# Two groups of TensorE transposes as pairs of half transposes in a hybrid SSD and attention layer

## The chip, the cores and the metric

The kernel runs on one core of a Trainium2 chip. The metric is device time in microseconds (us), the median of several executions; less is better. PE is TensorE's matmul side and PEld its loading of weights, DVE is VectorE, ACT is ScalarE, POOL is GpSimd, SP is the engine that issues the transfers here.

## The reference

One post-norm layer over 512 tokens of width 1024, in float32. Cut to what matters for the change:

```python
u = h @ w_in                        # z | x,B,C | dt | q | k | v | gates
xbc = silu(centred_conv(xbc))       # x: 2048 channels, B and C: 4 groups x 128
y_f = ssd_chunked(xh, dt_f, a_f, bm, cm)          # chunks of 128 tokens, 32 heads of 64
y_b = flip(ssd_chunked(flip(xh), flip(dt_b), a_b, flip(bm), flip(cm)))
y = (y_f + y_b + d_skip * xh) * silu(z)           # then a grouped RMS norm
mix = (gate_a * (y @ w_proj_ssd) + gate_b * (attention(q, k, v) @ w_proj_attn)) @ w_out
h = layer_norm(alpha * h + mix, ln1_g, ln1_b)     # the first norm
f = square(relu(h @ w_up)) @ w_down
h = layer_norm(alpha * h + f, ln2_g, ln2_b)
```

Inside `ssd_chunked`, the states of a chunk and the output within a chunk both contract over tokens, so they need x with tokens on the partitions. `h @ w_up` contracts over the 1024 channels, so it needs the first norm's output with channels on the partitions. Both arrays are produced the other way round, and TensorE transposes them.

## The kernel before

Large products are made of three matmuls of split operands (`mm3`, lines 120 to 127): a value is a rounded high part and a low remainder (ACT casts the high part, DVE subtracts it), and high x high (L124), the first operand's low part x high (L125) and high x the second operand's low part (L126) are summed in one bank of PSUM. Weights are streamed from DRAM by `Stream`: a transfer, a cast on ACT (L103) and a subtraction on DVE (L104) for every tile of weights, ahead of its use.

The work runs in stages. First comes the projection of v and dt. Then come four groups `g` of SSD heads: for each, a generator `ssd(g)` issues the state-space work and a second generator issues projection tiles of w_in (names B, C, x, z, q, k, g), and `run` interleaves the two by the numbers that they yield. On PE this order is kept as written (`manual_schedule`); the other engines get an order from the framework's scheduler, and each engine then carries out its own list strictly in order. After that come attention beside the SSD output projection, the output projection with the first norm, and the channel sublayer (up and down products).

The change touches two places. In `ssd(g)` (L385 to L393), each of the four chunks of 128 tokens takes one PSUM bank of the three with tag "tp", four transposes of 128 x 128 (one for each of the group's four x tiles, channels by tokens), and one copy on ACT into a tile `xt` of 512 columns; a yield of 1.0 stands between the chunks, so that other matmuls run there. `weigh` (L401) then multiplies a chunk's `xt` by decay weights on DVE (`xw`, L404), casts it on ACT (`xwh`, L407) and subtracts on DVE (`xwl`, L408); the state product `ps_st` on PE needs `xwh` for its first matmul and `xwl` for its second.

In `h1_transpose(i)` (L868 to L877), for the 128 tokens of tile i, four transposes go to a first bank (channels 0 to 511) and four to a second (channels 512 to 1023). For each bank ACT casts to `hth` (L876) and DVE subtracts into `htl` (L877). Lines 889 to 900 issue the output product and norm of the four tiles, these transposes, and `up_first(0)` to `up_first(3)`, which compute the first half of the tokens (tiles 0 and 1) for the first four blocks of w_up; the second half (tiles 2 and 3) follows in the loop at L917. Here the scheduler also orders PE, so `ps_u` (the up product) and `ps_ht` (the transposes) can be mixed.

A transpose is a matmul: the block is the stationary operand, the identity (the first 128 columns of `tri`) moves. In rows of the profile the moving operand stands before the stationary one, and the sizes are rows x columns of the weights, then rows x columns of the moving operand.

## Time and profile before

| What | Value |
|---|---|
| Median of 3 runs (lowest to highest) | 1035.73 us (1035.19 to 1036.61) |
| Profiled execution, own time | 1036.7 us |
| Span of its instructions | 1034.9 us |
| PE busy | 1018.9 us, 98% of the span |
| PEld, DVE, ACT, POOL busy | 82%, 63%, 49%, 7% |
| Transposes of x (L389) | 64, starting from 90.8 to 399.2 us |
| Transposes of the first norm's output (L873) | 32, starting from 667.1 to 688.4 us |

The profiled execution lasted 1.8 us more than its span, and 0.97 us more than the median. The duration of a matmul in a row runs from its start to its modelled end; matmuls are pipelined, so the distance from one start to the next is what one costs the engine, and it is shorter than the duration. A row of the timeline merges neighbours of one kind: start, time from the first start to the last end, engine, line, names, and the number of instructions (x8). A number in brackets is idle time of that engine before the row, with what ended it.

### The profile page before, as it was taken

How to read it: one execution, taken by the hardware profiler on the slowest of the kernel's cores; microseconds unless marked ns; L12 is line 12 of the kernel's file. 1: busy time of each engine (PE TensorE's matmuls, PEld its weight loads, DVE VectorE, ACT ScalarE, POOL GpSimd, SP SyncE). 2: the span in 40 equal slices, each digit the busy share in tenths (PEclk: the TensorE clock that was granted, in tenths of full speed). 3: DMA queues.
4: the chain of work that ended last, by engine and by line, in shares of the span. 5: the costliest groups of instructions: out<-in, count | busy, mean ns of one | idle time of the engine just before them, and what ended most of it. 6: DMA issues, size and time to landing. Idle time of an engine off the chain costs nothing.

```text
span 1034.9 us, 13695 instructions
## 1 busy us (share of the span) xinstructions
PE 1018.9 (98%) x5169; PEld 843.6 (82%) x5169; DVE 650.1 (63%) x1009; ACT 511.1 (49%) x1009; POOL 73.5 (7%) x66
## 2 busy tenths in 40 slices
PE   9999999999999999999899999999999999999997
PEld 7888888888888888888678787898888888888886
DVE  4296978689979897874886276844442334443346
ACT  4444877478758865984564334224332213433120
POOL 0000101221131022121000000000000000000000
PEclk9999999999999999999899999999999999999999
DMA  6444355425542654564753168312332333333322
GB/s 235 148 161 130 122 184 173 143 87 176 179 150 94 193 178 148 180 197 148 249 164 86 58 188 311 101 42 62 102 91 92 102 102 98 88 101 102 96 88 81
DMA packets 48305, 140.42 MB, mean 136 GB/s; under 512 B 6512, under 2 KB 7280, under 8 KB 47984
## 3 DMA queue, kind: packets, MB, share of 16 engines
q1 hardware_dynamic: 48240, 139.56, 43.0%
q8 instruction: 40, 0.66, 0.3%
q14 instruction: 25, 0.20, 0.1%
HBM read 128.25 MB, written 11.30 MB: 135 GB/s over the span
## 4 chain that ended last, share of the span: by engine, by line
PE 89%; DMA 4%; DVE 4%; ACT 2%; issue 1%; SPq 0%; DVEq 0%; ACTq 0%
PE ps_u L125 6%; PE ps_u L124 6%; PE ps_d L124 6%; PE ps_u L126 6%; PE ps_d L125 6%; PE ps_d L126 6%; PE ps_z L124 3%; PE ps_z L125 3%; PE ps_z L126 3%; PE ps_g L124 3%; PE ps_g L125 3%; PE ps_g L126 3%; PE ps_x L124 2%; PE ps_x L126 2%; PE ps_x L125 2%; PE ps_pa L124 2%
## 5 line engine op out<-in xcount | busy, mean ns | idle before, releaser
L104 DVE TENSOR_TENSOR wl<-wraw,wh 128x1024 fp32r<-128x1024 f32 (+1 forms) x166 | 202.5, 1223 | 240.7 <-ACT wh L103 233.7
L103 ACT CAST wh<-wraw 128x1024 fp32r<-128x1024 f32 (+1 forms) x166 | 172.2, 1040 | 261.0 <-PE ps_d L126 108.6
L125 PE MATMUL ps_u<-htl,wh 128*128 128x512 f32 (+1 forms) x288 | 105.1, 366 | 0.3 <-DVE htl L877 0.3
L126 PE MATMUL ps_u<-hth,wl 128*128 128x512 f32 (+1 forms) x288 | 105.1, 365 | 0.0
L124 PE MATMUL ps_u<-hth,wh 128*128 128x512 f32 (+1 forms) x288 | 104.5, 366 | 0.3 <-ACT hth L876 0.2
L125 PE MATMUL ps_d<-wl,fh 128*128 128x512 f32 (+1 forms) x272 | 102.5, 377 | 0.0
L124 PE MATMUL ps_d<-wh,fh 128*128 128x512 f32 (+1 forms) x272 | 102.4, 377 | 0.0
L126 PE MATMUL ps_d<-wh,fl 128*128 128x512 f32 (+1 forms) x272 | 102.4, 377 | 0.0
L125 PEld LDWEIGHTS ps_u<-htl,wh 128*128 128x128 f32 x288 | 54.3, 189 | 9.2 <-DVE htl L877 0.5
L124 PEld LDWEIGHTS ps_u<-hth,wh 128*128 128x128 f32 x288 | 53.9, 189 | 9.5 <-ACT hth L876 0.7
L126 PEld LDWEIGHTS ps_u<-hth,wl 128*128 128x128 f32 x288 | 54.3, 189 | 8.8
L126 PEld LDWEIGHTS ps_d<-wh,fl 128*128 128x128 f32 x272 | 51.2, 188 | 9.5
L124 PEld LDWEIGHTS ps_d<-wh,fh 128*128 128x128 f32 x272 | 51.2, 188 | 9.4
L125 PEld LDWEIGHTS ps_d<-wl,fh 128*128 128x128 f32 x272 | 51.2, 188 | 9.3
L124 PE MATMUL ps_pa<-yh,wh 128*128 128x512 f32 x128 | 53.1, 415 | 0.0
L441 DVE SCALAR_TENSOR_TENSOR U<-bc,acr,U 128x128 f32<-128x128 f32 x128 | 47.9, 409 | 6.1 <-ACT U L439 5.9
L124 PE MATMUL ps_g<-xh,wh 128*128 128x512 f32 x128 | 51.4, 402 | 0.0
L125 PE MATMUL ps_pa<-yl,wh 128*128 128x512 f32 x128 | 50.9, 397 | 0.2 <-DVE yl L543 0.2
L124 PE MATMUL ps_x<-xh,wh 128*128 128x512 f32 x128 | 50.9, 398 | 0.0
L124 PE MATMUL ps_z<-xh,wh 128*128 128x512 f32 x128 | 50.9, 398 | 0.0
L126 PE MATMUL ps_pa<-yh,wl 128*128 128x512 f32 x128 | 50.7, 396 | 0.0
L126 PE MATMUL ps_x<-xh,wl 128*128 128x512 f32 x128 | 49.9, 390 | 0.0
(257 smaller groups left out, 2194.7 us busy)
## 6 DMA issues: line engine op xcount, KB each, us to landing
wraw<-in_w_in_dram SPq DMA_DIRECT2D x68, 512.0 KB, 3.5
bc<-dr_acr SPq DMA_DIRECT2D x32, 512.0 KB, 4.3
wraw<-in_w_up_dram SPq DMA_DIRECT2D x32, 512.0 KB, 3.6
wraw<-in_w_dn_dram SPq DMA_DIRECT2D x32, 512.0 KB, 3.6
be<-dr_ear SPq DMA_DIRECT2D x32, 256.0 KB, 4.4
wraw<-in_w_ps_dram SPq DMA_DIRECT2D x16, 512.0 KB, 3.7
dr_gate<-g SPq DMA_DIRECT2D x16, 256.0 KB, 2.0
wraw<-in_w_out_dram SPq DMA_DIRECT2D x8, 512.0 KB, 4.8
```

The source lines that it names most:

```text
L103: act.copy(h[:, :width], r[:, :width])
L104: dve.tensor_sub(l[:, :width], r[:, :width], f32(h[:, :width]))
L124: pe.matmul(ps, lh, rh, start=(first and i == 0), stop=False)
L125: pe.matmul(ps, lh, rl, start=False, stop=False)
L126: ins = pe.matmul(ps, ll, rh, start=False, stop=(last and i == n - 1))
L441: dve.scalar_tensor_tensor(U[:, ch(c)], bcs[0][:, hh, ch(c)], acr[:, c, h:h + 1], U[:, ch(c)], op0=ALU.subtract, op1=ALU.min)
```

## The change

A helper takes a list of 128 x 128 blocks and two banks. Each block is transposed in two instructions: rows 0 to 63 against the upper left 64 x 64 of the identity into 64 columns of the first bank, then rows 64 to 127 against the lower right 64 x 64 into 64 columns of the second. The two halves use different rows of the array and different banks.

For x, two chunks are done at a time: 16 half transposes (8 blocks) in one run on PE, then two copies, each of which writes the 64-column halves of both chunks; a tile `xt` now holds two chunks, and is complete after both copies. The yield is 2.0 for two chunks. For the first norm's output, the 8 blocks of a token tile give 16 half transposes; a bank now holds all 1024 channels of 64 tokens, and each cast and subtraction covers 8 x 64 columns in place of 4 x 128.

```diff
+    def transpose_halves(outs, ins):
+
+        for n, block in enumerate(ins):
+            for q in range(2):
+                r = slice(q * 64, q * 64 + 64)
+                pe.transpose(outs[q][:, n * 64:n * 64 + 64], block[r, :], ident[r, r])
@@ ssd @@
-        for c in range(NCH):
-            ps = ps_tile("tp", f"ps_xt{g}_{c}", 3)
-            for j in range(4):
-                pe.transpose(ps[:, ch(j)], xs[j][:, ch(c)], ident)
-            xtok = sp.tile([P, S], F32, name=f"xt{g}_{c}", tag="xt", bufs=4)
-            act.copy(xtok, ps)
-            xt.append(xtok)
-            yield 1.0
+        for c in (0, 2):
+            pss = [ps_tile("tp", f"ps_xt{g}_{c + q}", 3) for q in range(2)]
+            transpose_halves(pss, [xs[j][:, ch(c + q)] for q in range(2) for j in range(4)])
+            xtok = sp.tile([P, 2, S], F32, name=f"xt{g}_{c}", tag="xt", bufs=2)
+            for q in range(2):
+                act.copy(xtok.rearrange("p c (j q d) -> p (c j) q d", q=2, d=64)[:, :, q, :], pss[q].rearrange("p (n d) -> p n d", d=64))
+            xt += [xtok[:, 0, :], xtok[:, 1, :]]
+            yield 2.0
@@ h1_transpose @@
+        pss = [bank(pso_b[i][q], f"ps_ht{i}{q}") for q in range(2)]
+        transpose_halves(pss, [h1[i][:, k * P:(k + 1) * P] for k in range(KT)])
         for q in range(2):
-            ps = bank(pso_b[i][q], f"ps_ht{i}{q}")
-            for k in range(4):
-                pe.transpose(ps[:, k * P:(k + 1) * P], h1[i][:, (q * 4 + k) * P:(q * 4 + k + 1) * P], ident)
-            hs = hth[:, q * 4:q * 4 + 4, ts_]
-            p3 = ps.rearrange("p (k s) -> p k s", k=4)
-            act.copy(hs, p3)
-            dve.tensor_sub(htl[:, q * 4:q * 4 + 4, ts_], p3, f32(hs))
+            hs = slice(ts_.start + q * 64, ts_.start + q * 64 + 64)
+            p3 = pss[q].rearrange("p (k s) -> p k s", k=KT)
+            act.copy(hth[:, :, hs], p3)
+            dve.tensor_sub(htl[:, :, hs], p3, f32(hth[:, :, hs]))
```

The instructions move at two places of which the prediction speaks. The numbers behind the names count the tiles that the program has allocated.

The first is ACT's list in the last group, g = 3, between the cast `bth` and the second `xwh`. `xt_0` to `xt_3` are the chunks' tiles (after the change `xt_0` holds chunks 0 and 1, and `xt_2` chunks 2 and 3), `sq` is the square of the last output of group 2, `wh` a weight cast and `g` a gate. Before:

```order
L371 CAST bth_3762<-ps_bt_3757 128x512
L391 COPY xt_0_3821<-ps_xt_0_3816 128x512
L354 ACTIVATE sq_3807<-y_94 128x512
L391 COPY xt_1_3828<-ps_xt_1_3823 128x512
L407 CAST xwh_0_0_3868<-xw_0_0_3866 128x512
L103 CAST wh_3855<-wraw_3723 128x1024
L304 ACTIVATE g_3836<-ps_g_3781,vec 128x512
L391 COPY xt_2_3844<-ps_xt_2_3839 128x512
L391 COPY xt_3_3851<-ps_xt_3_3846 128x512
L407 CAST xwh_1_3_3874<-xw_1_3_3872 128x512
```

And with the change:

```order
L378 CAST bth_3804<-ps_bt_3799 128x512
L361 ACTIVATE sq_3849<-y_94 128x512
L398 COPY xt_0_3876<-ps_xt_0_3858 128x8x64
L398 COPY xt_0_3876<-ps_xt_1_3859 128x8x64
L103 CAST wh_3911<-wraw_3765 128x1024
L311 ACTIVATE g_3885<-ps_g_3823,vec 128x512
L398 COPY xt_2_3906<-ps_xt_2_3888 128x8x64
L398 COPY xt_2_3906<-ps_xt_3_3889 128x8x64
L414 CAST xwh_0_0_3924<-xw_0_0_3922 128x512
L414 CAST xwh_1_3_3930<-xw_1_3_3928 128x512
```

The square moved ahead of the first copy, and the first `xwh` went from ahead of the weight cast, the gate and the last two copies to behind them.

The second is PE's list where the transposes of token tiles 1 and 2 meet the up product. `h_1` and `h_2` are the norm's outputs, `ps_u_0` to `ps_u_2` the first blocks of the up product. Before:

```order
L873 MATMUL ps_ht_6361<-tri,h_1_6007 128x128 x4
L873 MATMUL ps_ht_6418<-tri,h_2_6008 128x128 x2
L124 MATMUL ps_u_0_6368<-hth,wh_6032 128x256
L124 MATMUL ps_u_1_6393<-hth,wh_6077 128x256
L873 MATMUL ps_ht_6418<-tri,h_2_6008 128x128 x2
L873 MATMUL ps_ht_6425<-tri,h_2_6008 128x128 x4
L125 MATMUL ps_u_0_6368<-htl,wh_6032 128x256
```

And with the change:

```order
L122 MATMUL ps_ht_6490<-tri,h_2_6064 128x64
L122 MATMUL ps_ht_6491<-tri,h_2_6064 128x64
L131 MATMUL ps_u_0_6440<-hth,wh_6088 128x256
L131 MATMUL ps_u_1_6465<-hth,wh_6133 128x256
L131 MATMUL ps_u_2_6512<-hth,wh_6176 128x256
L132 MATMUL ps_u_0_6440<-htl,wh_6088 128x256
```

All half transposes of tile 2 now stand ahead of the first up matmuls, and three high x high matmuls stand ahead of the first one that needs `htl`, where there were two.

## The prediction

> **What bounds the kernel now.** I read the page first: which engine is busy, and what the chain of work that ended last is made of.

> ```profile
> PE 1018.9 (98%) x5169; PEld 843.6 (82%) x5169; DVE 650.1 (63%) x1009; ACT 511.1 (49%) x1009; POOL 73.5 (7%) x66
> PE 89%; DMA 4%; DVE 4%; ACT 2%; issue 1%; SPq 0%; DVEq 0%; ACTq 0%
> ```

> PE is busy for 98% of the span, and is 89% of the chain. So PE's own list sets the time: what it saves or spends on transposes counts in full, unless PE then meets something that comes from ACT or DVE. Two questions follow: what a run of half transposes costs PE, and where the later products of ACT and DVE make it wait. For the first I read the rows of the instructions, and the timeline of PE around three runs of matmuls: full transposes, fp32 matmuls with 64 rows in two alternating row halves (the attention scores, L621, which write two banks in turn as the changed code does), and matmuls whose moving operand is one column.

> ```profile
> L389 PEld LDWEIGHTS ps_xt<-tri,x x64: 137/140/143, 90.5 to 399.2; 128*128 128x128 f32 x64
> L330 PEld LDWEIGHTS ps_ms<-tri,sq x32: 187/192/192, 214.2 to 481.7; 128*128 128x128 f32 x32
> L621 PEld LDWEIGHTS ps_s<-k,q x64: 182/188/188, 522.6 to 538.3; 64*128 64x128 f32 x64
> L621 PE MATMUL ps_s<-k,q x64: 272/272/373, 522.7 to 538.4; 64*128 64x128 f32 x64
> ```

> ```profile
> 201.47 0.40 PE L125 MATMUL ps_z<-xl,wh 128*128 128x512 f32 x1
> 201.70 0.39 PE L126 MATMUL ps_z<-xh,wl 128*128 128x512 f32 x1
> 201.93 1.03 PE L389 MATMUL ps_xt<-tri,x 128*128 128x128 f32 x8
> 202.72 0.48 PE L124 MATMUL ps_z<-xh,wh 128*128 128x512 f32 x1
> 203.04 0.40 PE L125 MATMUL ps_z<-xl,wh 128*128 128x512 f32 x1
> ```

> An ordinary matmul of 512 columns steps by 0.23 us (201.47 to 201.70). From 201.70 to 203.04 are 1.34 us; without two such steps 0.88 us are left for 8 full transposes, 0.110 each. Seven steps and a duration of 0.27 make the row's 1.03 too, so nothing is paid for starting or stopping.

> ```profile
> 522.33 0.39 PE L126 MATMUL ps_pa<-yh,wl 128*128 128x512 f32 x1
> 522.65 1.16 PE L621 MATMUL ps_s<-k,q 64*128 64x128 f32 x16
> 523.74 0.50 PE L124 MATMUL ps_pa<-yh,wh 128*128 128x512 f32 x1
> 524.08 0.39 PE L125 MATMUL ps_pa<-yl,wh 128*128 128x512 f32 x1
> ```

> ```profile
> 523.31 0.50 PE L621 MATMUL ps_s<-k,q 64*128 64x128 f32 x6
> ```

> The last six of these sixteen (the second fence, a narrow window) take 0.50 us; less one duration of 0.272 the third pair starts 0.23 us after the first, so a pair steps by some 0.112 us: two halves of 64 rows run at once, in the time of one full matmul. But the whole run takes 1.75 us from 522.33 to 524.08, without the two ordinary steps 1.29, and 8 pairs are only 0.90 of it. **0.39 us is a fixed price** of going over to 64 rows and back, which the full transposes don't pay.

> **The change on PE.** 8 full transposes become 8 pairs of halves with 64 moving columns. The stream of a pair is half of 0.110, 0.055 us. Its weights still have 128 columns, so their loading can take its place as the bound:

> ```profile
> 312.31 0.39 PE L126 MATMUL ps_st<-xwh,btl 128*128 128x512 f32 x1
> 312.54 0.95 PE L330 MATMUL ps_ms<-tri,sq 128*128 128x1 f32 x8
> 313.35 0.49 PE L124 MATMUL ps_k<-xh,wh 128*128 128x512 f32 x1
> 313.67 0.40 PE L125 MATMUL ps_k<-xl,wh 128*128 128x512 f32 x1
> ```

> With one moving column, 8 matmuls still take 1.36 - 0.46 = 0.90 us, 0.112 each: that is what loading 128 fp32 columns costs (a load of 192 ns in its row). A transpose's load lasts 140 ns in its row, 52 ns less, which leaves 0.060. I take 0.060 us for a pair. Its bounds are 0.055 (the stream alone) and 0.112 (the pair of L621, whose 188 ns load has as many columns). The fixed price is taken at 0.34: the first pair's load can't run ahead under other matmuls (its row has durations up to 373 ns, 0.1 over the median), and such a load is 0.05 shorter here. Its bounds are none and 0.39. A run of 8 pairs then costs 0.34 + 8 x 0.060 = 0.82 us against 0.88, a gain of 0.06; by the bounds 0.44 to 1.29, a gain of 0.44 or a loss of 0.41. Halving the stream nearly pays for the change of mode, and no more.

> [...]

> There are 8 such runs for x (two in each group) and 4 for the norm's output. The gain counts only where PE doesn't meet a wait behind it, which holds for the six runs of groups 0 to 2 and for token tile 0: 7 x 0.06 = **0.4 us gained**.

> **The change behind PE.** ACT's copies and DVE's subtractions keep their number and elements. I take their durations as unchanged:

> ```profile
> L404 DVE TENSOR_TENSOR xw<-xt,wdec x24: 678/692/1415, 92.2 to 412.9; 128x512 f32<-128x512 f32 x24
> ```

> `xw` already goes through its tile in 8 runs of 64 columns, and its median of 692 ns is that of the plain subtraction `xwl` (0.69, below). The copies' bounds are a tenth of a microsecond either way, inside the forecast's own range. What changes is that a consumer needs both banks' copies where it needed one. Three places have little slack.

> Group 3, where the changed ACT list has the first `xwh` behind the weight cast, the gate and all four copies:

> ```profile
> 402.12 0.39 PE L124 MATMUL ps_st<-xwh,bth 128*128 128x512 f32 x1
> 402.35 0.39 PE L125 MATMUL ps_st<-xwl,bth 128*128 128x512 f32 x1
> ...
> 397.81 0.63 ACT L354 ACTIVATE sq<-y 128x512 f32<-128x512 f32 x1 [0.33 <-DVE y L352]
> ...
> 398.81 0.62 ACT L407 CAST xwh<-xw 128x512 fp32r<-128x512 f32 x1
> 399.33 1.05 ACT L103 CAST wh<-wraw 128x1024 fp32r<-128x1024 f32 x1
> 400.28 0.69 ACT L304 ACTIVATE g<-ps_g,vec 128x512 f32<-128x512 f32 x1
> 400.86 1.07 ACT L391 COPY xt<-ps_xt 128x512 f32<-128x512 f32 x2
> ...
> 403.34 0.69 DVE L408 TENSOR_TENSOR xwl<-xw,xwh 128x512 fp32r<-128x512 f32 x1 [0.69 <-ACT xwh L407]
> ```

> The square can't start before 397.81, since it waits for DVE. Two copies follow at 0.49 each (start to start; two take 1.07), then the cast, the gate and two more copies: these stand where they stood, so the last copy starts at 401.33, `xwh` at about 401.82 and ends at 402.44 instead of 399.43. `xwl` (0.69) ends at about 403.18. PE's second state matmul comes at 403.24 instead of 402.35: **0.9 us lost**, and the two runs' own gain in this group vanishes in it. Behind that matmul stand the rest of the state product and the gate tile's matmuls, which nothing else can bring forward. In groups 0 to 2 the same reckoning leaves slack; nearest to a wait is group 2:

> ```profile
> 303.93 0.39 PE L125 MATMUL ps_st<-xwl,bth 128*128 128x512 f32 x1
> ...
> 299.76 1.60 ACT L391 COPY xt<-ps_xt 128x512 f32<-128x512 f32 x3
> ```

> Four copies from 299.76 let `xwh` start at 301.7, and `xwl` ends at 303.1, for a matmul at 303.93.

> Token tile 1. The first up matmul that needs `htl` reads all 256 tokens of one channel block, which were in the first bank before and are now in both:

> ```profile
> 674.31 1.08 ACT L876 CAST hth<-ps_ht 128x512 fp32r<-128x512 f32 x2 [3.85 <-PE ps_ht L873]
> ...
> 674.94 0.51 PE L124 MATMUL ps_u<-hth,wh 128*128 128x256 f32 x2
> ...
> 675.67 0.67 DVE L877 TENSOR_TENSOR htl<-ps_ht,hth 128x512 fp32r<-128x512 f32 x1
> ...
> 676.38 0.64 DVE L877 TENSOR_TENSOR htl<-ps_ht,hth 128x512 fp32r<-128x512 f32 x1
> 676.40 0.39 PE L125 MATMUL ps_u<-htl,wh 128*128 128x256 f32 x1 [0.29 <-DVE htl L877]
> ```

> PE waited for the first subtraction (ended 676.34), and will wait for the second (677.02). The casts are done before either starts, so DVE's own list dates them, not PE: 0.67 us later, with one matmul of 0.12 done ahead in return, **0.55 us lost**; what tiles 1 and 2 gain on PE is lost in the same wait.

> Token tile 3, behind which PE has only up matmuls that read it:

> ```profile
> 687.78 1.03 PE L873 MATMUL ps_ht<-tri,h 128*128 128x128 f32 x8
> 689.05 1.21 PE L124 MATMUL ps_u<-hth,wh 128*128 128x256 f32 x6 [0.24 <-ACT hth L876]
> 690.10 0.28 PE L125 MATMUL ps_u<-htl,wh 128*128 128x256 f32 x1
> ...
> 688.41 1.07 ACT L876 CAST hth<-ps_ht 128x512 fp32r<-128x512 f32 x2 [11.44 <-PE ps_ht L873]
> ```

> The first cast started when 4 transposes had ended. Now it waits for 16 halves: 0.09 to enter, 0.11 to the second pair and 6 x 0.06 put the last start at about 688.34; its end, at the duration less half a stream (0.27 - 0.05), is 688.56, so the casts run from 688.58 to 689.65 instead of 689.00 for the first alone. PE comes at 689.71 instead of 689.05, **0.65 us lost**. `htl` is then not late: both subtractions end near 690.5, and PE wants them at 690.76.

> **The sum.** 0.9 + 0.55 + 0.65 - 0.4 = 1.7 us more than before. The profiled execution, 1034.9 of span and 1.8 around it, would go from 1036.7 to 1038.4; it stood 0.97 above the median, so against the median of 1035.73 the forecast is **1037.4 us**, with an own range of 1036.7 to 1038.1 as the slack of each wait is off by some tenths.

> **The rivals.** (1) A pair is bound by its weights, or by issue, as the L621 pair: 0.112 us. Then a run costs 1.29, the seven runs lose 7 x 0.41 = 2.9 instead of gaining 0.4, and tile 3's casts start 0.36 later still: 1035.73 + 2.9 + 0.36 + 2.1 = 1041.1 us. For it: loads of both kinds have 128 columns. Against it: the 50 ns between the two loads' rows. If halves in transpose mode did not overlap at all, a pair would cost two steps of 0.110, a run 2.15, and the time pass 1044 us; the overlap of L621 speaks against it.

> (2) Going over costs transposes nothing, and pairs run at 0.055. The seven runs gain 7 x 0.44 = 3.1, the waits stay at about 2.0: 1034.6 us. For it: the price of 0.39 is seen with loads twice as long. Against it: 522.33 to 522.65 is 0.09 over a step ahead of the first pair, and 523.74 to 524.08 is 0.11 over one behind the last, where the load is that of an ordinary matmul, as it will be. [...]

> (3) The waits don't bite: ACT gets its gate and casts earlier as PE moves, or something before dates PE. Then tile 3's 0.65 and the gain of 0.4 are all: 1036.0 us. For it: lists show order and not time. Against it: ACT's rows in group 3 follow without gaps.

> **How the numbers follow.** The forecast has 0.52, rival 1 0.20 (0.05 of it for no overlap at all), rival 2 0.13, rival 3 0.15. A measurement of this kernel tells 0.2% (2.07 us) from no change: slower begins at 1037.80, faster at 1033.66. Of the forecast's 0.52, some 0.20 lie above 1037.80, which with rival 1 gives slower 0.40; faster needs rival 2 with a wait missing, 0.05; the rest, 0.55, is no change. The range from 1034.9 to 1041.2 leaves out most of rival 2 and the far end of rival 1, 0.16 together.

> **What would show it.** In the profile after: half transposes in pairs that start together, and pairs 0.06 apart (rival 1: 0.11); 0.3 to 0.4 us of gaps around each run; PE idle of about a microsecond at `ps_st` of group 3 with `xwl` as its releaser, of 0.9 us or more at the first `htl` matmul, and near 0.8 us before the up matmuls behind tile 3. Without these three waits, or with runs that take well under 0.8 us, I am wrong.

## The result and the profile after

The changed kernel takes **1042.79 us** (median of 6 executions, 1042.08 to 1045.36), the kernel before 1036.69 us beside it: a ratio of **1.0069, 95% interval 1.0058 to 1.0081**, 6 to 8 us slower. The forecast was 1037.4 us with a range up to 1041.2, so the time lies outside it, on the slow side. The execution that was profiled lasted 1045.36 us (span 1043.6), the slowest of the six, so its trace shows up to 2.6 us more loss than the median has.

The first and fourth part of the page of the changed kernel:

```profile
PE 1023.5 (98%) x5265; PEld 843.0 (81%) x5265; DVE 649.1 (62%) x1009; ACT 510.5 (49%) x1009; POOL 73.8 (7%) x66
PE 90%; DVE 4%; DMA 3%; ACT 2%; issue 1%; POOL 0%; SPq 0%; DVEq 0%; ACTq 0%; POOLq 0%
```

PE is busy for 4.6 us longer than before, although its products are the same and only the transposes are cut in two. The waits of PE (engine, what it was about to do, on whom; total us, times, longest us) are new or longer than before at three places: on the copies of x (`ps_xt`, no such wait before), at the output projection (`ps_o`, 3.5 us in three waits where it was 1.5 in two) and at the up product (`ps_u <- ACT hth`, 0.2 before):

```profile
PE ps_o L131 <- ACT wh L103: 1.9, 1, 1.9
PE ps_u L131 <- ACT hth L882: 1.8, 2, 1.2
PE ps_xt L122 <- ACT xt L398: 1.7, 1, 1.7
PE ps_o L131 <- DVE mb L774: 0.8, 1, 0.8
PE ps_o L132 <- DVE wl L104: 0.8, 1, 0.8
```

I then followed the distance between the two traces: the start of the same matmul after, less its start before. It is 0.38 us at the first group, falls to 0.09 ahead of group 2, and then goes up in steps: +3.2 at group 2, +1.0 at group 3, +3.9 in the output projection (631 to 655 us), +1.3 at token tiles 1 and 3; 0.8 comes back at the wait in front of attention. In all it is 8.7 us at the end, which is the two spans' difference.

**The runs themselves are as forecast.** The timeline of PE around the first run of the changed kernel, and a narrow window of it from the third pair on:

```profile
90.92 0.39 PE L133 MATMUL ps_B<-xh,wl 128*128 128x512 f32 x1
91.23 0.71 PE L122 MATMUL ps_xt<-tri,x 64*128 64x64 f32 x16
91.88 0.50 PE L131 MATMUL ps_B<-xh,wh 128*128 128x512 f32 x1
92.22 0.40 PE L132 MATMUL ps_B<-xl,wh 128*128 128x512 f32 x1
```

```profile
91.41 0.54 PE L122 MATMUL ps_xt<-tri,x 64*128 64x64 f32 x12
```

From 90.92 to 92.22 are 1.30 us; without two ordinary steps of 0.227 the run costs 0.85, against 0.82 forecast and 0.88 for 8 full transposes. The last six pairs take 0.54; less one duration of 0.22 that is five steps of 0.06. The fixed price is 0.85 - 8 x 0.06, about 0.36 us.

**Group 2.** Here the changed kernel loses most by one wait. PE's transposes of group 2 before, and then PE and ACT at the same place after:

```profile
296.20 1.04 PE L389 MATMUL ps_xt<-tri,x 128*128 128x128 f32 x8
...
298.46 0.60 PE L389 MATMUL ps_xt<-tri,x 128*128 128x128 f32 x4
...
300.45 0.66 PE L389 MATMUL ps_xt<-tri,x 128*128 128x128 f32 x4
```

```profile
296.41 0.71 PE L122 MATMUL ps_xt<-tri,x 64*128 64x64 f32 x16
...
297.86 0.69 DVE L359 TENSOR_TENSOR y<-y,yt 128x512 f32<-128x512 f32 x1 [1.47 <-POOL yt L358]
298.58 0.63 ACT L361 ACTIVATE sq<-y 128x512 f32<-128x512 f32 x1 [1.25 <-DVE y L359]
298.63 0.27 PE L122 MATMUL ps_xt<-tri,x 64*128 64x64 f32 x1
299.12 1.04 ACT L319 ACTIVATE k<-ps_k 128x512 f32<-128x512 f32 x1
299.97 1.10 ACT L398 COPY xt<-ps_xt 128x512 f32<-128x512 f32 x2
300.64 1.08 PE L122 MATMUL ps_xt<-tri,x 64*128 64x64 f32 x15 [1.73 <-ACT xt L398]
301.65 0.79 PE L131 MATMUL ps_z<-xh,wh 128*128 128x512 f32 x1
302.24 0.63 PE L132 MATMUL ps_z<-xl,wh 128*128 128x512 f32 x1
302.67 0.63 PE L133 MATMUL ps_z<-xh,wl 128*128 128x512 f32 x1
```

The banks with tag "tp" are three, and the fourth chunk gets the bank of the first. Before, PE asked for it at 300.45, two microseconds after the third chunk. Now the second run alternates between the banks of chunks 2 and 3, so it needs both at 298.63. It gets through one half transpose, and then waits until ACT has copied chunk 0. In ACT's list that copy stands behind `sq`, which waits for DVE's `y`, and behind `k`. After this wait the matmuls are 0.43 us apart (302.24 to 302.67) and not 0.23. The windows of that stretch show why; the third number from the end is the granted clock:

```profile
297.30:300.72 3.42, 1.69 (x9) 1.02 (x10) 1.83 (x2) 2.17 (x5) 1.96 (x2) 1.00 0.35 97
300.72:304.13 3.41, 3.41 (x21) 2.81 (x22) 1.51 (x3) 1.94 (x4) 0.09 (x1) 0.50 0.92 268
```

For 3.41 us behind the wait the clock is granted at 0.50. I estimate that this costs 3.41 x (1 - 0.23 / 0.43) = 1.6 us at most, from the two distances between matmuls, and PE counts as busy in it.

**Group 3, token tiles 1 and 3** lose about what was forecast: 1.0 us in group 3, 0.55 us at tile 1 and 0.68 us at tile 3 by the distance between the two traces. PE's rows in group 3, and at tiles 1 and 3:

```profile
405.79 0.50 PE L131 MATMUL ps_st<-xwh,bth 128*128 128x512 f32 x1
406.51 0.50 PE L132 MATMUL ps_st<-xwl,bth 128*128 128x512 f32 x1 [0.22 <-DVE xwl L415]
...
683.05 0.50 PE L131 MATMUL ps_u<-hth,wh 128*128 128x256 f32 x2 [0.66 <-ACT hth L882]
683.82 0.38 PE L131 MATMUL ps_u<-hth,wh 128*128 128x256 f32 x1 [0.26 <-DVE htl L883]
684.49 0.39 PE L132 MATMUL ps_u<-htl,wh 128*128 128x256 f32 x1 [0.29 <-DVE htl L883]
...
697.70 1.20 PE L131 MATMUL ps_u<-hth,wh 128*128 128x256 f32 x6 [1.16 <-ACT hth L882]
```

**The output projection** is 200 us behind the changed code for x and ahead of that for the norm, and nothing in it was edited; SP issues the same transfers in the same order. Yet PE waits there 1.94 us for a cast weight whose transfer is late, and half clock follows (652.29 to 655.70 us):

```profile
650.20 0.50 PE L131 MATMUL ps_o<-wh,mixh 128*128 128x512 f32 x1 [1.94 <-ACT wh L103]
651.46 0.50 PE L132 MATMUL ps_o<-wl,mixh 128*128 128x512 f32 x1 [0.76 <-DVE wl L104]
```

### The profile page after: what moved, and what is told of

It reads as the page before. It is cut to its first block, busy times and chain, and to the rows that moved or that the text cites. A ratio compares the mean times of both kernels' runs of the same rounds, so it can differ in the third digit from the quotient of the medians.

```text
span 1043.6 us, 13887 instructions
## 1 busy us (share of the span) xinstructions
PE 1023.5 (98%) x5265; PEld 843.0 (81%) x5265; DVE 649.1 (62%) x1009; ACT 510.5 (49%) x1009; POOL 73.8 (7%) x66
## 4 chain that ended last, share of the span: by engine, by line
PE 90%; DVE 4%; DMA 3%; ACT 2%; issue 1%; POOL 0%; SPq 0%; DVEq 0%; ACTq 0%; POOLq 0%
PE ps_u L132 6%; PE ps_u L133 6%; PE ps_d L132 6%; PE ps_u L131 6%; PE ps_d L133 6%; PE ps_d L131 6%; PE ps_z L131 3%; PE ps_x L131 3%; PE ps_x L133 3%; PE ps_x L132 3%; PE ps_z L132 3%; PE ps_z L133 3%; PE ps_g L131 3%; PE ps_g L132 2%; PE ps_g L133 2%; PE ps_pa L131 2%
## 5 line engine op out<-in xcount | busy, mean ns | idle before, releaser
L103 ACT CAST wh<-wraw 128x1024 fp32r<-128x1024 f32 (+1 forms) x166 | 172.2, 1041 | 265.7 <-PE ps_d L133 108.6
L132 PE MATMUL ps_z<-xl,wh 128*128 128x512 f32 x128 | 50.3, 393 | 0.0
```

The source lines that it names most:

```text
L103: act.copy(h[:, :width], r[:, :width])
L132: pe.matmul(ps, lh, rl, start=False, stop=False)
```

## The experiments

The names used in the expectations: theory A is the late bank of group 2 with the half clock behind it; T is its part for the norm, the two waits at token tiles 1 and 3; P is that the half transposes themselves cost PE more than forecast; D is that the output projection's transfers make the loss; F came last and says that the transfers of PE's own instructions make them late. The rivals H (the halves themselves make the wait) and R (the loss is spread over the program) stand in single expectations. Ratios are to the kernel before on the same chip, with 95% intervals; medians of different rows come partly from different chips, so differences are taken between ratios. "x" is the part in `ssd`, "norm" the part in `h1_transpose`.

| Run | Kernel | Median (range), us | Ratio |
|---|---|---|---|
| after | the change | 1042.79 (1042.08 to 1045.36) | 1.0069 (1.0058 to 1.0081) |
| e1 | norm only | 1038.62 (1036.38 to 1042.39) | 1.0022 (1.0011 to 1.0034) |
| e2 | x only | 1043.77 (1040.36 to 1046.99) | 1.0073 (1.0055 to 1.0091) |
| e3 | x only, fourth bank elsewhere | 1040.54 (1038.80 to 1041.62) | 1.0040 (1.0026 to 1.0055) |
| e4 | x only, four chunks in one run | 1035.74 (1033.02 to 1040.76) | 0.9997 (0.9984 to 1.0011) |
| e5 | full transposes in the change's order | 1037.55 (1036.19 to 1042.31) | 1.0011 (0.9999 to 1.0023) |
| e6 | before, x's rows late | 1034.43 (1033.54 to 1035.00) | 0.9972 (0.9962 to 0.9982) |
| e7 | the change, x's rows late | 1040.51 (1038.72 to 1042.44) | 1.0035 (1.0022 to 1.0049) |
| e8 | e4, x's rows late | 1033.18 (1032.41 to 1035.31) | 0.9966 (0.9953 to 0.9979) |
| f1 | e7, fourth bank elsewhere | 1037.17 (1034.41 to 1039.94) | 1.0001 (0.9988 to 1.0013) |
| f2 | norm only, x's rows late | 1036.23 (1033.69 to 1038.73) | 0.9987 (0.9976 to 0.9999) |
| f3 | norm for tiles 0 and 2 only, x's rows late | 1034.40 (1033.40 to 1036.02) | 0.9975 (0.9965 to 0.9985) |
| f4 | x only, x's rows late | 1040.34 (1038.17 to 1046.11) | 1.0034 (1.0020 to 1.0048) |
| g1 | before, 64 matmuls more at the start | 1037.81 (1035.28 to 1042.42) | 1.0018 (1.0002 to 1.0033) |
| g2 | the change, 64 more | 1040.42 (1037.36 to 1044.84) | 1.0044 (1.0027 to 1.0062) |
| g3 | e3, 64 more | 1035.68 (1034.76 to 1037.49) | 0.9994 (0.9984 to 1.0004) |
| g4 | before, 32 more | 1037.41 (1035.81 to 1040.10) | 1.0013 (1.0004 to 1.0023) |

### Which part, and is it the bank (e1 to e4)

e1 keeps the loop over chunks as it was; e2 keeps `h1_transpose` as it was. e3 is e2 with another bank for the fourth chunk:

```diff
-            pss = [ps_tile("tp", f"ps_xt{g}_{c + q}", 3) for q in range(2)]
+            pss = [ps_tile(*(("y", f"ps_xt{g}_3", 2) if c + q == 3 else ("tp", f"ps_xt{g}_{c + q}", 3))) for q in range(2)]
```

e4 has e3's banks, and issues both calls of `transpose_halves` first (32 half transposes in one run), then all four copies, then one `yield 4.0`.

> Only the transposes of the first norm's output are halves; those of x are as before. Theory A (waits: a late PSUM bank and the clock that it lowers in the x part, two casts in place of one in the norm part): the norm part costs the two waits that the profile after shows at token tiles 1 and 3, 0.75 + 0.55 - 0.06 = 1.2 us, so 1.1 to 1.5 us over the kernel before, with no idle PE before 600 us that the kernel before does not have. Rival P (the half transposes themselves cost PE more than the full ones, whatever waits): 4 of the 12 runs are here, so a third of the whole 6 us, 2 us. Rival D (the late transfers in the output projection, 3.9 us in the profile after, are the cost, and come from any shift of the work): 3 us or more.

> Only the transposes of x are halves; the first norm's are as before. Theory A: PE waits 2.0 us in group 2 for the fourth bank, which is free only when ACT has copied the first, the clock then falls to half for a window of 3.4 us (1.2 us lost), and group 3 loses 0.9 us in two waits, against 0.3 gained in the runs: 3.5 to 4.5 us over the kernel before, and the profile shows the wait for ACT xt inside the second run of group 2. Rival P: two thirds of 6 us, 4 us, but spread evenly over the four groups. Rival D: the loss comes mostly after 600 us.

> As the run with only x halved, but the second half bank of the second run of each group is one of the two banks of tag y, which are free there, so that no bank waits for a copy of the same group. PE's instructions and their order are the same. Theory A: the 2.0 us wait and the 1.2 us of low clock in group 2 are gone, and 0.35 of group 3; what stays is group 3's wait for xwl (0.5 to 0.9) less the 0.3 of the runs: 0 to 0.6 us over the kernel before. Rival P: no change against the run with only x halved, 4 us over the kernel before.

> Only x halved, with the banks of the run before, and all four chunks of a group in one run of 32 half transposes; the copies and a yield of 4.0 follow. The fixed price of a run is paid once in a group instead of twice. By the forecast's price (0.34 fixed, 0.060 a pair) a group costs 1.30 us against 1.76 for 16 full transposes, and with ACT's list having the first xwh ahead of the weight cast in group 3 no wait is left: 1.8 us under the kernel before. Rival P: 2 us or more over the kernel before. If the fixed price grew with the run: no difference.

The x part alone loses as much as the whole change (0.69%), and the norm part alone another 0.22% (e1), so the two don't add up. e2 lost 0.73%, some 7.5 us, where theory A had 3.5 to 4.5: its trace has 4.9 us ahead of the output projection and 3.3 in it. Taking the bank's wait away (e3) brings back 0.33% of it, 3.4 us; in its trace the wait and the half clock of group 2 are gone, and the distance to the kernel before falls by 0.3 us across group 2 where it rose by 4.6 in e2. So theory A holds for group 2. e1's loss of 0.22% (0.11 to 0.34) has room for the 1.1 to 1.5 us expected, but its trace has a wait that the expectation excluded. With x as before, and full transposes, PE waits for the copy of the first chunk too:

```profile
PE ps_xt L396 <- ACT xt L398: 1.1, 1, 1.1
```

f2, further down, has 0.9 us of it, and the traces of before and e6 have none. So the bank of the fourth chunk was already at its limit: the rows of before leave 0.1 us between the end of the first copy (299.76 and about 0.6) and PE's start at 300.45. The change asks for the bank two microseconds sooner.

P falls: e4 has as many half transposes as e2 and none of its loss; ahead of attention's wait its trace is 1.9 us ahead of before, because four chunks in one run pay the fixed price once (e8 has the same runs: from 91.37 to 93.16 us, without two steps of 0.227, one takes 1.34 us, against 1.76 for 16 full transposes), and because the first `xwh` of group 3 stands ahead of the weight cast on ACT again. The median doesn't show the forecast gain of 1.8 us, though: e4 equals before within 0.16%. And e3 is still 4 us slower than before, where theory A left 0 to 0.6, and its trace puts 4.6 us into the output projection:

```profile
PE ps_o L131 <- ACT wh L103: 3.8, 1, 3.8
```

That left D open.

### The order with full transposes, and the transfers of the output projection (e5 to e8)

e5 is the kernel before with two chunks in one run, all transposes full:

```diff
+        for c in (0, 2):
+            pss = [ps_tile("tp", f"ps_xt{g}_{c + q}", 3) for q in range(2)]
+            for q in range(2):
+                for j in range(4):
+                    pe.transpose(pss[q][:, ch(j)], xs[j][:, ch(c + q)], ident)
+            for q in range(2):
+                xtok = sp.tile([P, S], F32, name=f"xt{g}_{c + q}", tag="xt", bufs=4)
+                act.copy(xtok, pss[q])
+                xt.append(xtok)
+            yield 2.0
```

In e6 to e8 the four loads of x's rows for the residual no longer stand among the output projection's weights. A write of 8 columns, from a weight that arrives late, makes them wait:

```diff
@@ after the loop over k that streams the weights @@
-        dma.dma_start(h1[k], t["x"][k * P:(k + 1) * P, :])
+        if k == 2:
+            gate = w[1]
+    for k in range(4):
+        pool.tensor_copy(h1[k][:, 0:8], f32(gate[:, 0:8]))
+        dma.dma_start(h1[k], t["x"][k * P:(k + 1) * P, :])
```

> The kernel before, with the eight transposes of two chunks of x issued as one run on PE into two banks of the three-buffer set and the two copies behind them, as the change does, but every transpose stays a full 128 x 128 one. Theory A (what costs the changed kernel time at group 2 is that the second run needs its second bank before ScalarE has copied the first chunk, and the granted clock that falls behind that idle time; the halves themselves are harmless): the same idle time of about 2 us in front of the second run of group 2, one stretch of 3.4 us at half clock behind it, and about 0.4 us in group 3; the median goes from 1036.6 to 1039 to 1041 us. Rival H (the halves, or the two-chunk copy that follows them, make the wait): no idle time there over 0.5 us and a median within 1 us of the kernel before.

> The kernel before, with the four loads of x's rows for the residual (tile h, 512 KB each) held back until the second of the output projection's streamed weights has been split, so that they queue behind the weights and not ahead of them. One element block of each row tile is first written by GpSimd from that weight, only to make the load wait. Theory D (the waits in the output projection are weights that queue behind these loads): the wait of 0.73 us for the cast weight disappears, the one of 0.77 us for its remainder stays or shrinks, and the median falls by 0.5 to 1.5 us to about 1035.5 us. Rival (the queue of transfers is not the cause): within 0.5 us of before.

> The changed kernel with the same four loads held back in the same way. Theory D (2 to 4 us of the change's loss are the output projection's late weight, which comes later in most executions of the changed kernel, and the half clock behind it): the wait of 1.9 us and the stretch of half clock in that stage disappear, and the median falls from 1042.8 to about 1040 us; its distance to the other kernel with the loads held back is then about 4.8 us, the sum of what the trace shows at group 2 (3.2), group 3 (1.0), token tiles 1 and 3 (1.2), less the 0.8 that the wait in front of attention takes back. Rival (the output projection's loss has another cause than this queue): the wait stays and the median is within 1 us of 1042.8.

> x alone in halves, all four chunks of a group in one run of 32 pairs of halves, the fourth chunk's bank from the other set of banks (as in the run of four chunks before), and the four loads of x's rows held back as in the two runs beside it. Theory A with D: no late bank, no late weight: the median is about 1 us under the one with the four-chunk run alone (1035.7), 1034 to 1035 us, and the spread of its times (1033.0 to 1040.8 there) becomes smaller. Rival: the spread has another source and stays, with a median of 1035 to 1036 us.

In e5 the wait is there with full transposes too, as theory A says:

```profile
297.82 0.60 PE L390 MATMUL ps_xt<-tri,x 128*128 128x128 f32 x4
299.93 0.66 PE L390 MATMUL ps_xt<-tri,x 128*128 128x128 f32 x4 [1.51 <-ACT xt L393]
```

It is the two banks in one run, and not the halves, that make it: in the order of before PE comes to the fourth chunk 2.0 us after the third (298.46 to 300.45), which here is at about 299.8, just when the bank is free. But no half clock followed this wait in this execution, and the median is at most 0.23% up, under the 1039 us that A had forecast: A overrated what the wait alone costs. The trace of e5 also loses 2.4 us in the output projection, half clock included, although it has as many PE instructions as before.

e6 gains 0.28%, 2.9 us, more than the 0.5 to 1.5 expected: the wait of 0.7 us for the cast weight is gone, that for its remainder is down to 0.2, and the times spread over 1.5 us only.

```profile
PE ps_o L125 <- DVE wl L104: 0.2, 1, 0.2
```

So in the kernel before the queue costs time as well. But e7 gains about as much over the changed kernel (0.34%), and stays 0.63% behind e6, as the change is 0.69% behind before; its median is near the 1040 us expected, and its distance to e6, 6.1 us, is not the 4.8 of the expectation. The loads of x's rows are a cost that both kernels share; D in this form doesn't explain the difference. e8 was expected at 1034 to 1035 us and is faster still, and its five times lie within 2.9 us of each other, where e4's twelve spread over 7.7.

### Both parts with the bank's wait gone, and the norm tile by tile (f1 to f4)

f1 is e7 with e3's bank, f2 is e1 and f4 is e2, each with x's rows late as in e6. f3 is f2 with the old form (`h1_full`, the function of the kernel before) for the odd tiles:

```diff
     def h1_transpose(i):
+        if i in (1, 3):
+            return h1_full(i)
```

> The whole change (both parts in halves) with the loads of x's rows held back, and the fourth chunk of a group in a bank of the other set, so that no run of x waits for ScalarE's copy of the first chunk. The same without that bank change took 1040.5 us, the kernel before with the rows held back 1034.4. Theory A (the late bank of group 2 is the largest single loss, 1.5 to 3.1 us of idle time by execution and up to 1.7 us of half clock behind it): no idle time before the second run of group 2, and a median of 1036.5 to 1037.5 us, which is 1034.4 plus 1.0 (group 3), plus 1.2 (token tiles 1 and 3), less 0.3. Rival R (the remainder of the 6.1 us is spread over the program and not at that bank): above 1039 us.

> Only the norm's output in halves, x as before, the loads of x's rows held back. Theory T (the two waits for the split at token tiles 1 and 3 are all that this part costs): PE waits of 0.66 and 1.16 us for the projection up, and a median of 1034.4 + 1.2 = 1035.6 us. Rival (this part disturbs more than these two waits): above 1036.5 us.

> The norm's output in halves for token tiles 0 and 2 alone, tiles 1 and 3 as before, x as before, the loads of x's rows held back. Theory T: no wait for the split that is not there before, median 1034.4 us within 0.3, about 1.2 us under the one with all four tiles in halves. Rival (the halves of any tile cost): half of the loss stays, about 1035 us.

> Only x in halves, with the banks of the changed kernel, the norm's output as before, the loads of x's rows held back. Theory A: the idle time of 1.5 us or more before the second run of group 2 is there, group 3 loses 1.0, and the median is the one of both parts less the norm part's 1.2 us, 1039.3 us. Rival (the x part is harmless once the output projection's weights are on time): under 1037 us.

f1 against e7 gives the bank of group 2 its price again: 0.34%, 3.5 us, as e3 against e2. Its median is inside the interval that A forecast. The idle time itself was 1.73 us in the changed kernel, 3.09 in e2, 1.50 in e7 and 2.15 in f4, since DVE comes to `y` sooner or later, and half clock followed in three of the four (the section on the clock, at the end, tells more). f4 came out at 1040.34 us for 1039.3. And f1's trace, of one of its slower executions, still loses 4.3 us at the output projection, to which the section on g1 to g4 returns.

For the norm, f2 less e6 is 0.15%, 1.6 us, and f3 less e6 is 0.03%: tiles 0 and 2 cost nothing that shows, and tiles 1 and 3 make the difference. The intervals of f2 and f3 overlap (0.9976 to 0.9999, 0.9965 to 0.9985), so this rests on the waits more than on the medians. f2's are the forecast ones, and f3's are those of before:

```profile
PE ps_u L131 <- ACT hth L887: 1.8, 2, 1.2
...
PE ps_u L132 <- DVE htl L888: 0.3, 1, 0.3
PE ps_u L131 <- DVE htl L888: 0.3, 1, 0.3
```

```profile
PE ps_u L132 <- DVE htl L889: 0.4, 1, 0.4
...
PE ps_u L131 <- ACT hth L888: 0.2, 1, 0.2
```

f2 was expected at 1035.6 and is 0.6 above; a stretch of half clock behind tile 1's wait in its trace (677.09 to 680.50 us) is in line with that.

### Where PE's own program arrives (g1 to g4)

By now eight kernels with x in halves had been profiled. Against before or e6, their traces lose 3.3 to 4.6 us at the output projection in five cases (after, e2, e3, f1, f4), 1.3 in e7, and 0.6 and 0.7 in e4 and e8; those with only the norm in halves lose 0.5 at most, e5 2.4. Up to the end of this stage's products the lists of SP, ACT and DVE are the same as before there, and so is PE's but for the norm's transposes. What differs is in the DMA view. The page has a second kind of transfer, PE's instructions (queue; packets, MB, share of 16 engines), of the kernel before:

```profile
q8 instruction: 40, 0.66, 0.3%
```

These are 16 KB each, and between one and the next PE carries out 255 instructions in the mean, counting weight loads, which makes about 64 bytes each (16,384 / 255). x in halves has 64 matmuls and 64 weight loads more, half of such a block, so the later transfers of instructions come about half a block earlier. Before, they start at 622.6 and 654.0 us; after, at 612.2 and 646.1, which is 122 and 92 instructions earlier, the transposes of x not counted. The DMA view of the kernel before from 627 to 648 us, then of the changed kernel from 631 to 648:

```profile
q1 hardware_dynamic: 1874, 6.86, 90.5%
```

```profile
q1 hardware_dynamic: 1525, 5.44, 88.2%
q8 instruction: 1, 0.02, 0.3%
```

One transfer of instructions, 0.93 us long, then falls into the stretch where the data transfers take 88 to 91% of the engines. And ahead of it, in the kernel before, the transfer at 622.6 coincides with an issue by SP that takes 1.75 us and not 0.32 as after (a gate tile at 622.56). The issue behind it, the 1 MB of the layer norm's parameters, starts that much later; the parameters land within 4.6 us, and in the changed kernel within 7.5. The DMA view's issues, before and after (last column: us to landing):

```profile
ln<-in_ln_dram SPq DMA_DIRECT2D x1, 1024.0 KB, 4.6
```

```profile
ln<-in_ln_dram SPq DMA_DIRECT2D x1, 1024.0 KB, 7.5
```

In the five profiles with x's loop as before it is 4.6 to 5.7 us (5.5 in e5), in the eight with halves 6.1 to 8.1. The test puts instructions whose products nothing reads ahead of everything, and makes all matmuls of the warm-up smaller, so that it takes about as long (WARM is 11):

```diff
-    for _ in range(WARM):
-        pe.matmul(ps_w, warm[:, :P], warm, start=True, stop=True)
+    for _ in range(WARM + 64):
+        pe.matmul(ps_w[:32, :72], warm[:, :32], warm[:, :72], start=True, stop=True)
```

g4 has `WARM + 32` and 128 columns.

> The kernel before, with 64 more matmuls in the warm-up ahead of the first product: 75 of 72 columns in place of 11 of 512, about the same time in all, on zeros that nothing reads. Theory F: PE's program arrives as transfers of 16 KB, one for every 256 of its instructions (weight loads counted), each about 1 us on one of the 16 DMA engines. In the kernels with x as before, one falls at 622 and the next at 654 us, on either side of the stretch from 627 to 645 us in which the output projection's weights queue behind each other; the halves of x add 128 instructions ahead of it, half of such a block, and put one into the stretch, at 640 to 647. So the same 128 instructions, added at the start here, put a transfer of instructions between 636 and 648 us, the layer norm's parameters land 6 to 8 us after their issue and not 4.7, PE waits 2 us or more in the output projection, and the median goes from 1036.7 to 1038.5 to 1040 us. Rival (where PE's program arrives makes no difference): within 0.7 us of the kernel before.

> The changed kernel with the same 64 matmuls more in the warm-up, which with the 128 instructions of the halves of x make one whole block of 256: the transfers of instructions fall at about 626 and 657 us, as in the kernel before. Theory F: the waits in the output projection shrink from 3.5 us to 1.5 us as before, without half clock behind them, and the median falls from 1042.8 to 1040 us (1039.3 to 1040.8). Rival: it stays within 0.7 us of 1042.8.

> x alone in halves with the fourth chunk's bank from the other set (1040.54 us, of which its profile showed 4.6 us in the output projection), with the 64 matmuls more in the warm-up. Theory F: the output projection's loss goes, and the median falls to 1037.0 to 1038.0 us (1036.7, plus 1.0 for group 3, less 0.3, give or take). Rival: 1040 us or more.

> The control for the warm-up: the kernel before, with 32 matmuls more (43 of 128 columns). This moves the transfers of instructions by a quarter of a block, from 622 and 654 us to about 615 and 647 us. Theory F: both lie outside the stretch in which the weight that PE waits for is under way (638 to 643 us), so the median stays within 0.7 us of 1036.7. If the altered warm-up itself costs time, this kernel is slower by as much as the one with 64.

The two kernels change places at the output projection. The waits there, and the landing of the layer norm's parameters, of g1 (the kernel before with 64 more):

```profile
PE ps_o L124 <- ACT wh L103: 2.8, 1, 2.8
```

```profile
ln<-in_ln_dram SPq DMA_DIRECT2D x1, 1024.0 KB, 7.0
```

and of g2 (the change with 64 more):

```profile
PE ps_o L131 <- ACT wh L103: 0.8, 1, 0.8
```

```profile
ln<-in_ln_dram SPq DMA_DIRECT2D x1, 1024.0 KB, 4.8
```

In g1 the transfer of instructions starts at 642.4 us and the distance to before grows by 3.9 us in this stage, half clock included, in g2 at 624.9 and 656.4 and it grows by 0.1, where the change had 3.9. g2 is 0.25% faster than the change, as forecast (1040.4 for 1040), and g3 is 0.46% faster than e3, more than forecast (1035.7 for 1037 to 1038). The first product starts at 6.0 to 6.5 us in these four traces and at 5.8 to 6.3 in the others, so the altered warm-up itself costs some tenths at most. It is the same in g1, g2 and g3, and it costs the kernel before time where it saves the other two some. So in these three runs what is lost at the output projection went with the place of the instruction transfers; of the three, g3 is far outside the noise, and g1 and g2 are just outside it.

How a transfer of instructions makes the weights late is not shown. Two expectations were missed. g1 rose by 0.18% only (0.02 to 0.33), 1.3 us above before, 0.7 below the forecast interval; its times reach from 1035.3 to 1042.4. And g4, meant as a control, rose by 0.13%, at the edge of what was expected: with transfers at 614.6 and 647.4 us the parameters land after 7.6 us too, and PE waits 1.79 us. Other traces speak against the transfer inside the stretch as the cause. e4 and e8 have one there (638.5 and 636.5 us) and lose 0.6 and 0.7 us. f1 has one at 641.8 us, but its long wait ends at 633.0 us, well ahead of that. PE waits there for DVE's `mb`, whose gate tile SP loads behind the layer norm's parameters, and half clock follows:

```profile
PE ps_o L131 <- DVE mb L774: 2.0, 1, 2.0
```

What goes together in all 18 traces is the other end. In seven (before, e5, e6, f2, f3, g2, g3) a transfer of instructions starts within 0.8 us ahead of SP's issue just before the parameters, or together with it (0.01 us later, in before), that issue takes 0.88 to 1.75 us, and the parameters land within 4.6 to 5.5 us. In the other eleven no transfer starts there in time (e1's comes 0.09 us after the issue's start), the issue takes 0.32 us, and the parameters land within 5.7 to 8.1. Even so, e5 loses 2.4 us with 5.5, and e8 loses 0.7 with 7.3. Which of these things makes the waits long was not separated.

## Why the prediction was wrong, point by point

**The cost of a run was right.** A pair steps by 0.06, the fixed price is 0.36 and a run 0.85 us: 0.03 and not 0.06 gained per run. Rival 1 (0.11 a pair) and rival 2 (0.44 a run) are out. That rival 1's 1041.1 us is nearer to the measured time than the forecast is chance.

**Group 3 and token tiles 1 and 3 were right**: 1.0 us for the 0.9 forecast, and 0.55 and 0.68 for 0.55 and 0.65. The way differs a little. In group 3 the two state matmuls are 0.72 us apart and not 0.23, half of the wait of about a microsecond that was to be seen; the rest came mostly before, when the second run waited 0.39 us for a bank there as well. e3, which doesn't wait for that bank, loses the same 1.0 us, so `xwl` sets it, as forecast. At tile 1 the first wait is 0.66 us for both casts, and then two short ones for `htl`. With f2, the norm's part is 1.6 us in the median, 0.4 over the two waits. Rival 3 (waits that don't bite) is out.

**The step that failed is the one on the slack of groups 0 to 2**: "In groups 0 to 2 the same reckoning leaves slack; nearest to a wait is group 2". That reckoning followed the copies forward, to `xwh`, `xwl` and the state product. It never asked what the run needs in order to start. With two banks taken at once out of three, the second run of each group needs the bank of the first chunk, and the rows for it were in the profile of before: ACT's first copy of group 2 at 299.76, and PE's transposes of the third chunk at 298.46, with which those of the fourth were now to run. The 1.3 us between them, and the copy's own half microsecond, were to be read off; what the forecast put at nothing is a wait of 1.73 us, and half clock behind it. The runs priced it at 3.4 to 3.5 us in the median (e2 to e3, e7 to f1), idle time and half clock together. It is the pairing of two chunks that takes both banks at once, as e5's wait of 1.51 us with full transposes shows.

**Two terms were missing altogether.** The first is the half clock: behind PE's wait of 1.73 us the clock was granted at 0.50 for 3.41 us, which I estimate at up to 1.6 us more. The second is what the added instructions do at the output projection, which went with where the instruction transfers fall: moving these by half a block took back 2.6 us of the change's time (g2), and 4.8 of the part for x with its bank moved (e3 to g3). The sum counted the time of the added instructions, and not their transfer (41 transfers of 16 KB where there were 40). Beside the forecast, the chances were shared among three rivals about the runs and the waits that it names; none had a wait at another place.

**The accounts.** The late bank 3.5, the instructions 2.6, group 3 1.0, the norm's two tiles 1.6, less 0.2 saved (the seven runs), make 8.5 us against 7.1 by the ratio (0.69% of 1036.7). Each of the differences between two medians is uncertain by about 2 us, and the terms meet in the same queue, so they need not add up more closely than that. That g1 costs the kernel before only 1.3 us where g2 gives back 2.6 stays open.

## What to carry to other kernels

When operations are joined into one run, ask two things of every buffer: who needs the products now (later), and when the run now needs its buffers (earlier); the second is read from the row of whoever frees them. Halves of 64 rows cost about 0.36 us for each excursion here, so runs of 8 pairs gained next to nothing (0.85 us against 0.88), and one of 16 pairs in e8 gained 0.42 (1.34 against 1.76). With four chunks in a run, another bank for the fourth and x's rows out of the weights' way, e8 took 1033.18 us, 0.34% under the kernel before; e6 has 0.28% by the loads alone, and the 0.06% between them is within the noise. Where a stage waits for transfers without slack, as the output projection here, a change of some hundred instructions ahead of it can move it by microseconds (4.8 us from e3 to g3); a shift by matmuls that nothing reads, put at the start, helps to tell that from the change's own cost.

## What the hardware showed that was not expected

```profile
644.63:648.04 3.41, 0.67 (x2) 0.35 (x3) 1.44 (x2) 2.09 (x2) 0.00 (x0) 1.00 0.63 198
648.04:651.45 3.41, 3.41 (x9) 2.65 (x10) 2.18 (x2) 1.05 (x1) 0.00 (x0) 0.50 0.71 209
```

```profile
673.67:677.09 3.42, 2.21 (x27) 1.67 (x24) 3.42 (x8) 2.28 (x5) 0.00 (x0) 1.00 0.00 0
677.09:680.50 3.41, 3.41 (x18) 3.41 (x17) 2.81 (x4) 0.00 (x0) 0.00 (x0) 0.50 0.10 34
```

So in these traces the limit, but for f2's window, lies between 1.6 and 2 us of idle time in a window, and a wait of that size cost up to 1.6 us more, by the estimate above, or nothing more, by where it fell on the grid: g2's wait at group 2 was longer than the change's, 2.30 us, but lay across two windows, with 1.62 in the first, and no half clock followed. The times of f2 show both (six at 1035.9 us or less with a mean clock of 0.996, six at 1036.6 or more with 0.993 to 0.994). Why f2's 1.21 us sufficed is open.

**The two halves of a pair overlap almost entirely.** They start 3 to 9 ns apart and last 0.22 to 0.27 us each (in the run at 91.23 us), so the 0.06 us from pair to pair is the price of both.
